# Six blocks of a two-layer trunk take four Strassen pairs in a row instead of one and then two, and one mixer block fetches its decay rows with priority

## The chip, the cores and the metric

The kernel runs on one core of a Trainium2 chip. The metric is the time of one launch in microseconds (us) on the device, the median of three runs. The core has TensorE (PE: matmuls; PEld: its weight loads), VectorE (DVE), ScalarE (ACT), GpSimd (POOL) and SyncE (SP). DMA transfers are issued from queues of SP, POOL and ACT and share 16 DMA engines.

## The reference

256 tokens of width 2048 pass through two layers in fp32. Layer 0 has a combined input projection whose columns feed an mLSTM group (8 heads) and a Mamba-2 group (32 heads), then one output projection. Layer 1 is attention with rotary embedding, 16 heads. Each layer ends in a SwiGLU FFN of width 5632. Cut to the shape of it:

```python
p = rms_norm(x, g1) @ w_in               # q, k, v, o, gates, z, xBC, dt
x = x + concat(mlstm(p), ssd(p)) @ w_out # layer 0
h = rms_norm(x, g2)
x = x + (silu(h @ w_gate) * (h @ w_up)) @ w_down
q, k, v = split(rms_norm(x, g3) @ w_qkv) # layer 1
x = x + attention(rope(q), rope(k), v) @ w_o
h = rms_norm(x, g4)
x = x + (silu(h @ w_gate2) * (h @ w_up2)) @ w_down2
out = rms_norm(x, g5)
```

## The kernel before

All large products have the activations on one side (256 tokens, two tiles of 128) and a weight matrix read from HBM on the other. Both sides are split into a high part (a cast to the matmul's type) and a low part (the number minus its high part), and a product is three matmuls: high by high, high by low, low by high (L311, L312, L313). So each weight tile passes ACT (cast into `wh`, L278) and DVE (low part into `wl`, L283).

The unit of work is `block()`: two strips of 512 columns by 2048 rows, as eight pairs of 256 rows. A pair is done in one of two ways, by its letter in `PLAN`:

- **P**, plain: two raw tiles of 512 KB (`raw`, issued on SP at L270 and L274), two casts, two low parts, 24 matmuls of 128x512.
- **S**, Strassen (Winograd's form): seven products of three matmuls, 21. Besides the first raw tile (L270) and a half-size second one (L272) it needs a tile of weight sums (`sums`): two plain copies on SP (L268), and behind each an accumulating copy on POOL's queue (L269). DVE adds the sums into the second raw (L293), and that into half of the first (L295). Casts and low parts are made of the first raw (a), the sums (s), the second raw (b) and the half (t). The matmuls go in the order of the products 2, 1, 3, 7, 5, 6, 4; the first two use a, the third b.

An S pair also needs sums of its activations: `activation_sums` (four subtractions on DVE, L246 to L249, into `sf`), then a split of `sf` into the tile `sk` (cast on ACT at L145, low part on DVE at L146). They are made when the activations are turned (`transpose_split`), where the list of a tensor names the pair, and else when first asked for (`summed`).

The pools set how far the weights run ahead (`SPACE`): six `raw`, two `sum`, six `wh`, six `wl`. The copies of a sums tile are tied behind the first raw load of five pairs earlier. Weights are emitted at a raised priority of 800. The order of the instructions on each engine is set when the program is built, by a scheduler that goes by priorities and dependences; on the chip each engine and each queue keeps that order.

The blocks follow each other so: bc (two), xz0 to xz3 (Mamba's x and z), qk0, w1 (half of the output projection), v0, o0, qk1, v1, o1, w2, the FFN, av0, aq0, aq1, av1, aq2, aq3 (values, and queries with keys, of layer 1), wo, the FFN. `o` is the plan of both o0 and o1; `aq` that of aq0 to aq3. From here on S4 is pair 4 of a block done as S, P7 pair 7 done as P.

While one block's matmuls run, small tasks of the stage before (`later`, run by `tick`) are put between the pairs: the mLSTM's chunks, the scan, attention's heads. From a block's first S to its last no such task is started. Among them `fetched_rows` (L657) reads decay rows back from a scratch tensor in HBM: two copies into a tile `rows`, on POOL's queue, or on ACT's (`nc.scalar`) where a caller says so. DVE adds masks to them (L671), ACT takes their exponents (L676, L677). Matmuls p_xs (L716) and p_y (L746) belong to that scan.

Of the kernel before, what the change touches and what calls it, by code (L numbers as in the profile page):

```python
# [17 lines left out]
P = 128  # L18
T = 256
# [16 lines left out]
SPACE = {"raw": 6, "sum": 2, "wh": 6, "wl": 6, "xa": 8, "sk": 3, "s": 10, "vh": 2, "ph": 1}  # L36
PLAN = {
    "bc": "PPPPPPPP", "xz": "PPPPPPPP", "qk0": "PPPPPPPP", "w1": ("PSPSPSPP", "PSPSPSSP"),
    "v0": "PPPSPSSP", "o": "PPPSPSSP", "qk1": "PPPSPSSP", "v1": "PPPSPSSP", "w2": ("PPPSPSPP", "PPPSPSSP"),
    "x": "PSPSPSSP", "x0": "PPPSPSSP", "down4": ("PSPSPSSP", "PSPSPSSP"), "down3": ("PSPSPP", "PSPSPP"),  # L40
    "av0": "PPPSPSSP", "aq": "PPPSPSSP", "av1": "PPPSPSSP", "wo": ("PPPPPPPP", "PPPSPSSP"),
}


# [17 lines left out]
def hybrid_trunk(ctx: ExitStack, tc: tile.TileContext, a: dict, out: bass.AP):  # L62
    nc = tc.nc
# [16 lines left out]
    def home(tag):  # L80
        return lambda shape, name, dt=F32: big.tile(shape, dt, tag=tag, name=name, bufs=SPACE[tag])

    xa_home, sk_home, s_home, vh_home = home("xa"), home("sk"), home("s"), home("vh")
    ph_home = home("ph")

    def t2(shape, name, dt=F32):
        return tmp.tile(shape, dt, tag="tmp", name=name, bufs=9)
# [42 lines left out]
    G_MIX0, G_FFN0, G_MIX1, G_FFN1, G_ML, G_SS, G_CB = 0, 16, 32, 48, 64, 80, 96  # L130
# [32 lines left out]
    def later(wait, name, fn, *args):  # L163
        pending.append((clock[0] + wait, len(pending), name, fn, args))
# [21 lines left out]
    def need(name):  # L186
        if any(q[2] == name for q in pending):
            assert not held[0], name
            run_until(lambda p: not any(q[2] == name for q in pending))
# [198 lines left out]
    def gathered(F, pre):  # L388
        for i in (0, 2, 1, 3):
            if pre is None:  # L390
                yield i // 2, i % 2, F[i]
            else:
                with tc.high_priority(offset=1600):
                    added[0] = (nc.vector.tensor_sub if i == 2 else nc.vector.tensor_add)(pre[i], F[i], pre[i]).ins
                yield i // 2, i % 2, pre[i]

    def sumsq(acc, src):
        j = t2([P, src.shape[-1]], "sq")
        nc.scalar.activation(j, src, AF.Square, accum_out=acc)
# [30 lines left out]
    def first_pair(src, turns_after, warm):  # L430
        raw = []
        for w, col in src:
            raw.append(home("raw")([P, 2, STRIP], "raw"))
            for k in range(2):
                nc.sync.dma_start(raw[-1][:, k, :], w[k * P:(k + 1) * P, col:col + STRIP])
        b = xt0.pair(0)
        pt = aux_bank("p_tr")
        with tc.issue_after(turns_after):
            for i in range(2):
                for t in range(NT):  # L440
                    turned = nc.tensor.transpose(pt[:, i * T + t * P:i * T + (t + 1) * P],
                                                 xin[t][:, i * P:(i + 1) * P], ident).ins
        with tc.issue_after(turned):
            warm_up(warm)
        pair = pt.rearrange("p (a b) -> p a b", a=2)
        high = [home("wh")([P, 2, STRIP], "wh", F32R) for _ in raw]
        low = [home("wl")([P, 2, STRIP], "wl", F32R) for _ in raw]

        def staged(s, k):
            with tied(last[0], cast[0]):  # L450
                split(high[s][:, k, :], low[s][:, k, :], raw[s][:, k, :])
            cast[0], last[0] = fresh

        for k in range(2):
            g = pv[:, G_MIX0 + k:G_MIX0 + k + 1]
            with tied(last[0], cast[0]) if k else ExitStack():
                split(b[:, k, 0, :], b[:, k, 1, :], pair[:, k, :], g)
            cast[0], last[0] = fresh
            staged(0, k)
        for k in range(2):  # L460
            staged(1, k)
        return [[(h[:, k, :], l[:, k, :]) for k in range(2)] for h, l in zip(high, low)]
# [57 lines left out]
    with tc.high_priority(offset=2000):  # L520
        first = first_pair(((w_in, C_B), (w_in, C_C)), rows_turned, WARM[1])
# [72 lines left out]
    scr = drp.tile([SH + MH, T], F32, name="scr")  # L594
# [65 lines left out]
    def fetched_rows(first, home, queue=nc.gpsimd):  # L660
        need("gates")
        rb = home([P, 2, W3], "rows2")
        for lo, l0, n in ((0, 0, T), (T, P, P)):
            queue.dma_start(rb[:, :, lo:lo + n],
                            bass.AP(tensor=scr.tensor, offset=scr.offset + first * T + l0,
                                    ap=[[0, P], [T, 2], [1, n]]))
        return rb

    def masked(rb):
# [49 lines left out]
    def ssd_rows(s, j, y, zg, wait=1):  # L719
        rows = fetched_rows(MH + 8 * s + 2 * j, s_home if j % 2 else sk_home, nc.scalar if s == 3 else nc.gpsimd)  # L720
        later(wait, ("y", s), ssd_decay, s, j, rows, y, zg)
# [188 lines left out]
    def next_x(name, gcol, sums, waits=(1, 2, 1, 2)):  # L910
        nx = KT("x" + name, KD, xa_home, sums)
        nx.sums = {j: None for j in sums}
        ss = cst.tile([P, NT, 4], F32, name="ss" + name)

        def done(s):
            cs = slice(s * STRIP, (s + 1) * STRIP)
            turn_strip(nx, s, [xr_[t][:, cs] for t in range(NT)], gcol, waits[s])
            for t in range(NT):
                sumsq(ss[:, t, s:s + 1], xr_[t][:, cs])

        return nx, ss, done
# [58 lines left out]
            down(hT, first, n, first + n == DFF // STRIP)  # L980
            first += n

    xt2, ss2, finish_ffn0 = next_x("2", G_MIX1, {3: sk_home, 5: sk_home, 6: sk_home})
    ffn(xt1, r1, a["l0_ffn_gate"], a["l0_ffn_up"], a["l0_ffn_down"], "a", finish_ffn0)


# [13 lines left out]
    aq, av, prob = {}, {}, {}  # L1000

    def rope_block(g, plan):
        F, pre = block(((w_qkv, g * STRIP), (w_qkv, D + g * STRIP)), xt2, 0, plan)
        tok = {}
        for t, i, src in gathered(F, pre):
            rot = t2([P, STRIP], "rot")
            both = src.rearrange("p (h f) -> p h f", f=HALF)
            nc.vector.tensor_mul(rot.rearrange("p (h f) -> p h f", f=HALF), both,
                                 rope[:, t, 0:1, :].to_broadcast([P, 8, HALF]))
            swp = t2([P, STRIP], "swp")  # L1010
            s4 = src.rearrange("p (h e f) -> p h e f", e=2, f=HALF)
            nc.vector.tensor_mul(swp.rearrange("p (h e f) -> p h e f", e=2, f=HALF), s4[:, :, ::-1, :],
                                 rope[:, t, None, 1:3, :].to_broadcast([P, 4, 2, HALF]))
            nc.vector.tensor_add(rot, rot, swp)
            tok[i, t] = rot
        for i in range(2):
            aq[g, i] = (vh_home if i == 0 else s_home)([P, 4, T], f"aq{i}")
        for i in (1, 0):
            for j in range(2):
                later(2, ("aq", g), qk_pair, aq[g, i][:, 2 * j:2 * j + 2, :],  # L1020
                      [tok[i, t][:, j * T:(j + 1) * T] for t in range(NT)])
        for hh in range(4):
            later(3 + hh // 2, ("oh", g, hh // 2), attend, g, hh)

    def values(g, plan):
        F, pre = block(((w_qkv, 2 * D + 2 * g * STRIP), (w_qkv, 2 * D + (2 * g + 1) * STRIP)), xt2, 0, plan)
        for i in range(2):
            av[2 * g + i] = s_home([P, NT, STRIP], f"av{i}")
        for t, i, src in gathered(F, pre):
            with tc.high_priority(offset=1600 if pre is None else 400):  # L1030
                nc.scalar.activation(av[2 * g + i][:, t, :], src, AF.Copy, scale=r2[:, t:t + 1])
# [42 lines left out]
            split(ob[:, hh % 2, 0, :], ob[:, hh % 2, 1, :], po[:, :T])  # L1074

    values(0, PLAN["av0"])
    rope_block(0, PLAN["aq"])
    rope_block(1, PLAN["aq"])
    values(1, PLAN["av1"])
    rope_block(2, PLAN["aq"])  # L1080
    rope_block(3, PLAN["aq"])
    xt3, ss3, done3 = next_x("3", G_FFN1, {1: vh_home, 3: vh_home, 5: sk_home, 6: ph_home})

    project(a["l1_w_o"], 0, oT, PLAN["wo"], done3)
# [110 lines left out]
```

## Time and profile before

| | us |
|---|---|
| median of 3 runs | 2530.19 (2529.63 to 2530.41) |
| profiled execution | 2527.28 |
| its span | 2525.3 |
| TensorE busy | 2514.8 (100%) |
| its weight loads busy | 2088.2 (83%) |
| DVE busy | 2237.2 (89%) |
| ACT busy | 1593.5 (63%) |
| POOL busy | 360.7 (14%) |
| mean granted clock | 0.999 |

The span runs from the first to the last instruction that the profiler saw; the profiled execution's time has 2.0 us around it and lies 2.9 us under the median of the runs. Busy times of engines overlap. A matmul's busy time counts from its start to its modelled end, and the next one starts before that, so TensorE's rate is read from starts.

### The profile page before, as it was taken

How to read it: one execution, taken by the hardware profiler on the slowest of the kernel's cores; microseconds unless marked ns; L12 is line 12 of the kernel's file. 1: busy time of each engine (PE TensorE's matmuls, PEld its weight loads, DVE VectorE, ACT ScalarE, POOL GpSimd, SP SyncE). 2: the span in 40 equal slices, each digit the busy share in tenths (PEclk: the TensorE clock that was granted, in tenths of full speed). 3: DMA queues.
4: the chain of work that ended last, by engine and by line, in shares of the span. 5: the costliest groups of instructions: out<-in, count | busy, mean ns of one | idle time of the engine just before them, and what ended most of it. 6: DMA issues, size and time to landing. Idle time of an engine off the chain costs nothing.

```text
span 2525.3 us, 34564 instructions
## 1 busy us (share of the span) xinstructions
PE 2514.8 (100%) x11553; PEld 2088.2 (83%) x11553; DVE 2237.2 (89%) x2984; ACT 1593.5 (63%) x2161; POOL 360.7 (14%) x444
## 2 busy tenths in 40 slices
PE   9999999999999999999999999999999999999998
PEld 8888888888888888888888888888888888888887
DVE  6877788978789999999999989988899999999998
ACT  6566666576767666566566666657666656665665
POOL 2101101121111111111111111110011111111110
PEclk9999999999999999999999999999999999999999
DMA  8656669878788999999999878776689999999995
GB/s 283 186 168 185 198 198 263 269 226 263 216 233 249 287 266 282 281 289 263 287 282 283 263 235 243 239 225 208 194 249 279 266 285 282 273 277 290 296 265 180
DMA packets 335362, 631.52 MB, mean 250 GB/s; under 512 B 27288, under 2 KB 31904, under 8 KB 335184
## 3 DMA queue, kind: packets, MB, share of 16 engines
q1 hardware_dynamic: 278960, 527.71, 61.8%
q0 software_dynamic: 52864, 98.18, 22.0%
q10 hardware_dynamic: 3360, 3.42, 0.5%
q8 instruction: 91, 1.49, 0.2%
q14 instruction: 87, 0.71, 0.1%
HBM read 627.07 MB, written 2.14 MB: 249 GB/s over the span
## 4 chain that ended last, share of the span: by engine, by line
PE 97%; DVE 1%; DMA 1%; ACT 0%; issue 0%; SPq 0%; POOL 0%; POOLq 0%; DVEq 0%; ACTq 0%
PE acc_f L311 24%; PE acc_f L313 24%; PE acc_f L312 24%; PE acc_e L311 6%; PE acc_e L313 6%; PE acc_e L312 6%; PE p_tr L178 1%; PE p_y L746 1%; PE p_qt L178 0%; PE p_o L178 0%; PE p_num L836 0%; DVE wl L283 0%; ACT wh L278 0%; PE p_qk L1038 0%; DMA raw<-in_l_w_in 0%
## 5 line engine op out<-in xcount | busy, mean ns | idle before, releaser
L278 ACT CAST wh<-raw 128x1024 fp32r<-128x1024 f32 (+1 forms) x1084 | 1047.2, 982 | 646.4 <-PE acc_f L313 278.4
L283 DVE TENSOR_TENSOR wl<-raw,wh 128x1024 fp32r<-128x1024 f32 (+1 forms) x1084 | 1208.8, 1135 | 161.3 <-ACT wh L278 151.1
L311 PE MATMUL acc_f<-wh,x 128*128 128x512 f32 x1168 | 457.5, 392 | 0.0
L313 PE MATMUL acc_f<-wh,x 128*128 128x512 f32 x1168 | 455.1, 390 | 0.0
L312 PE MATMUL acc_f<-wl,x 128*128 128x512 f32 x1168 | 454.8, 389 | 0.0
L278 ACT CAST wh<-sums 128x1024 fp32r<-128x1024 f32 x174 | 182.9, 1051 | 148.5 <-PE acc_f L313 72.5
L311 PE MATMUL acc_f<-wh,xa 128*128 128x512 f32 x678 | 269.6, 398 | 0.1
L313 PE MATMUL acc_f<-wh,xa 128*128 128x512 f32 x678 | 264.9, 391 | 0.0
L312 PE MATMUL acc_f<-wl,xa 128*128 128x512 f32 x678 | 264.6, 390 | 0.1
L313 PEld LDWEIGHTS acc_f<-wh,x 128*128 128x128 f32 x1168 | 219.2, 188 | 46.2
L312 PEld LDWEIGHTS acc_f<-wl,x 128*128 128x128 f32 x1168 | 219.4, 188 | 45.0
L311 PEld LDWEIGHTS acc_f<-wh,x 128*128 128x128 f32 x1168 | 219.3, 188 | 44.7
L283 DVE TENSOR_TENSOR wl<-sums,wh 128x1024 fp32r<-128x1024 f32 x174 | 212.3, 1220 | 31.8 <-ACT wh L278 30.9
L311 PE MATMUL acc_e<-wh,sk 128*128 128x512 f32 x522 | 203.6, 390 | 0.1
L312 PE MATMUL acc_e<-wl,sk 128*128 128x512 f32 x522 | 203.6, 390 | 0.0
L313 PE MATMUL acc_e<-wh,sk 128*128 128x512 f32 x522 | 203.4, 390 | 0.0
L269 POOL DMA_DIRECT2D sums<-in_l_ffn_gate x86 | 74.3, 864 | 773.1 <-DMA sums<-in_l_ffn_up 363.1
L313 PEld LDWEIGHTS acc_f<-wh,xa 128*128 128x128 f32 x678 | 127.3, 188 | 27.2
L312 PEld LDWEIGHTS acc_f<-wl,xa 128*128 128x128 f32 x678 | 127.5, 188 | 25.9 <-DVE wl L283 0.5
L311 PEld LDWEIGHTS acc_f<-wh,xa 128*128 128x128 f32 x678 | 127.3, 188 | 25.0 <-ACT wh L145 0.3
L293 DVE TENSOR_TENSOR raw<-raw,sums 128x512 f32<-128x512 f32 x174 | 119.3, 685 | 13.6 <-DMA sums<-in_l_ffn_down 7.5
L295 DVE TENSOR_TENSOR raw<-raw 128x512 f32<-128x512 f32 x174 | 119.5, 687 | 2.0
(334 smaller groups left out, 4034.4 us busy)
## 6 DMA issues: line engine op xcount, KB each, us to landing
raw<-in_l_ffn_gate SPq DMA_DIRECT2D x176, 512.0 KB, 6.2
raw<-in_l_w_in SPq DMA_DIRECT2D x175, 512.0 KB, 4.7
raw<-in_l_ffn_down SPq DMA_DIRECT2D x136, 512.0 KB, 6.8
raw<-in_l_ffn_up SPq DMA_DIRECT2D x90, 512.0 KB, 5.8
sums<-in_l_ffn_up SPq DMA_DIRECT2D x172, 256.0 KB, 5.0
raw<-in_l_w_qkv SPq DMA_DIRECT2D x78, 512.0 KB, 6.0
raw<-in_l_w_out SPq DMA_DIRECT2D x52, 512.0 KB, 6.0
sums<-in_l_ffn_gate POOLq DMA_DIRECT2D x86, 256.0 KB, 6.6
```

What stands on the lines that cost most here:

```text
L178: chain[kind] = put(*args, **kw).ins
L269: nc.gpsimd.dma_start(sums[:, i, :], other, accum_op=OP.add)
L278: cast[0] = nc.scalar.copy(h[:, :n, :], of[:, :n, :]).ins
L283: last[0] = nc.vector.tensor_sub(l[:, :n, :], of[:, :n, :], h[:, :n, :].bitcast(F32)).ins
L293: nc.vector.tensor_add(b[:, 1, :], b[:, 0, :], sums[:, 0, :])
L295: nc.vector.tensor_add(a[:, 0, :], a[:, 0, :], b[:, 1, :])
L311: nc.tensor.matmul(dst, ah, bh, start=start, stop=False, **kw)
L312: nc.tensor.matmul(dst, ah, bl, start=False, stop=False, **kw)
L313: nth[0] = nc.tensor.matmul(dst, al, bh, start=False, stop=stop, **kw).ins
L746: nc.tensor.matmul(py[:, o0:o0 + SHD], e[:, lo:lo + P], y[:, st, hs], start=st == 0, stop=st == t, skip_group_check=True)
```

## The change

It has three edits. The plans of o (two blocks), v1, av0, aq0 and aq2 get an S in the place of the P of pair 4, so that pairs 3, 4, 5 and 6 are S in a row. Since the blocks of layer 1 now differ, `aq` is written out as aq0 to aq3. The activations of layer 1's attention get a home for the sums of pair 4, so that these are made when the activations are turned. And `fetched_rows` gives its copies a priority of 1200 where they go on ACT's queue, which the last of the x and z blocks (xz3) does.

```diff
@@ PLAN
-    "v0": "PPPSPSSP", "o": "PPPSPSSP", "qk1": "PPPSPSSP", "v1": "PPPSPSSP", "w2": (...),
+    "v0": "PPPSPSSP", "o": "PPPSSSSP", "qk1": "PPPSPSSP", "v1": "PPPSSSSP", "w2": (...),
-    "av0": "PPPSPSSP", "aq": "PPPSPSSP", "av1": "PPPSPSSP", ...
+    "av0": "PPPSSSSP", "aq0": "PPPSSSSP", "aq1": "PPPSPSSP", "av1": "PPPSPSSP",
+    "aq2": "PPPSSSSP", "aq3": "PPPSPSSP", ...
@@ fetched_rows
         for lo, l0, n in ((0, 0, T), (T, P, P)):
-            queue.dma_start(rb[:, :, lo:lo + n], ...)
+            with tc.high_priority(offset=1200 if queue is nc.scalar else 0):
+                queue.dma_start(rb[:, :, lo:lo + n], ...)
@@
-    xt2, ss2, finish_ffn0 = next_x("2", G_MIX1, {3: sk_home, 5: sk_home, 6: sk_home})
+    xt2, ss2, finish_ffn0 = next_x("2", G_MIX1, {3: sk_home, 4: vh_home, 5: sk_home, 6: sk_home})
```

At the end `rope_block(0, PLAN["aq"])` and its three sisters become `rope_block(0, PLAN["aq0"])` and so on.

What this moves on the engines is shown at three places. First SP's queue in o0, before, from P4's two raws on: P4, S5's raws, S6's sums, S6's raws, P7 (L268 x2 are the two plain copies of one tile of sums).

```order
L270 DMA raw<-in_l_w_in 128x2x512
L274 DMA raw<-in_l_w_in 128x2x512
L270 DMA raw<-in_l_w_in 128x2x512
L272 DMA raw<-in_l_w_in 128x512
L268 DMA sums<-in_l_w_in 128x512 x2
L270 DMA raw<-in_l_w_in 128x2x512
L272 DMA raw<-in_l_w_in 128x512
L270 DMA raw<-in_l_w_in 128x2x512
L274 DMA raw<-in_l_w_in 128x2x512
```

The same queue at that place now: S4's raws, S5's raws, S5's sums, S6's raws, S6's sums, P7.

```order
L270 DMA raw<-in_l_w_in 128x2x512
L272 DMA raw<-in_l_w_in 128x512
L270 DMA raw<-in_l_w_in 128x2x512
L272 DMA raw<-in_l_w_in 128x512
L268 DMA sums<-in_l_w_in 128x512 x2
L270 DMA raw<-in_l_w_in 128x2x512
L272 DMA raw<-in_l_w_in 128x512
L268 DMA sums<-in_l_w_in 128x512 x2
L270 DMA raw<-in_l_w_in 128x2x512
L274 DMA raw<-in_l_w_in 128x2x512
```

S5's sums stood further up before, and S6's stood ahead of S6's raws; now S5's stand there, and S6's behind S6's raws.

Second DVE in av0, before: the first row ends the sums of pair 6's activations (`sk`). Behind it stand the rest of S5 and all of S6, with the split of pair 7's activations (`x_13601`) in between; P7 is next.

```order
L146 TENSOR_TENSOR sk<-sf,sk 128x4x128
L295 TENSOR_TENSOR raw<-raw 128x512
L283 TENSOR_TENSOR wl<-sums,wh 128x1024
L283 TENSOR_TENSOR wl<-raw,wh 128x1024
L283 TENSOR_TENSOR wl<-raw,wh 128x512
L293 TENSOR_TENSOR raw<-raw,sums 128x512
L283 TENSOR_TENSOR wl<-raw,wh 128x1024
L146 TENSOR_TENSOR x_13601<-xg,x_13601 128x2x256
L295 TENSOR_TENSOR raw<-raw 128x512
L283 TENSOR_TENSOR wl<-sums,wh 128x1024
L283 TENSOR_TENSOR wl<-raw,wh 128x1024
L283 TENSOR_TENSOR wl<-raw,wh 128x512
```

DVE in av0 now, from S6's first addition on:

```order
L293 TENSOR_TENSOR raw<-raw,sums 128x512
L283 TENSOR_TENSOR wl<-sums,wh 128x1024
L295 TENSOR_TENSOR raw<-raw 128x512
L283 TENSOR_TENSOR wl<-raw,wh 128x1024
L283 TENSOR_TENSOR wl<-raw,wh 128x512
L283 TENSOR_TENSOR wl<-raw,wh 128x1024 x2
L247 TENSOR_TENSOR sf<-xg 128x128
L283 TENSOR_TENSOR wl<-raw,wh 128x1024 x2
L248 TENSOR_TENSOR sf<-xg,sf 128x128
L146 TENSOR_TENSOR x_13655<-xg,x_13655 128x2x256
L249 TENSOR_TENSOR sf<-xg,sf 128x128
L146 TENSOR_TENSOR sk<-sf,sk 128x4x128
```

Three of the four subtractions of pair 6's activation sums and their split (`sk`, last row), and the split of pair 7's activations (`x_13655`), stand behind S6, P7 (the first x2) and aq0's first pair (the second x2). Before they stood ahead of S5's rest and within S6. On TensorE 12 matmuls of S6 and 14 of P7 follow that last split.

Third ACT's queue at the end of xz3, where the row fetches are issued (L664 before, L665 now; L696 and L697 of before are L697 and L698 now). Before:

```order
L664 DMA rows_2937<-scr 128x2x256
L696 ACTIVATE thz<-acc_f,rh_553 128x512
L697 ACTIVATE zg<-acc_f,rh_553 128x512
L278 CAST wh<-raw 128x1024
L148 ACTIVATE sx_2913<-p_tr,pv 128x256
L278 CAST wh<-raw 128x1024
L664 DMA rows_2937<-scr 128x2x128
L148 ACTIVATE sx_2913<-p_tr,pv 128x256
L664 DMA rows_3004<-scr 128x2x256
L664 DMA rows_3004<-scr 128x2x128
L278 CAST wh<-raw 128x1024
L479 ACTIVATE cv<-p_cv,convb,phase 128x256 x2
```

And now:

```order
L665 DMA rows_2937<-scr 128x2x256
L697 ACTIVATE thz<-acc_f,rh_553 128x512
L698 ACTIVATE zg<-acc_f,rh_553 128x512
L665 DMA rows_2937<-scr 128x2x128
L665 DMA rows_3077<-scr 128x2x256
L665 DMA rows_3077<-scr 128x2x128
L278 CAST wh<-raw 128x1024 x2
L148 ACTIVATE sx_2913<-p_tr,pv 128x256
L665 DMA rows_3004<-scr 128x2x256
L665 DMA rows_3004<-scr 128x2x128
L665 DMA rows_3135<-scr 128x2x256
L665 DMA rows_3135<-scr 128x2x128
```

The fetches of the first two tiles stand together ahead of two casts of weights, and those of the other two follow a few rows on; before, a cast, a split (L148) and another cast stood between the two copies of the first tile.

More of the change, by code (lines that the diff above doesn't have):

```diff
@@ L38 @@
     "bc": "PPPPPPPP", "xz": "PPPPPPPP", "qk0": "PPPPPPPP", "w1": ("PSPSPSPP", "PSPSPSSP"),
-    "v0": "PPPSPSSP", "o": "PPPSPSSP", "qk1": "PPPSPSSP", "v1": "PPPSPSSP", "w2": ("PPPSPSPP", "PPPSPSSP"),
+    "v0": "PPPSPSSP", "o": "PPPSSSSP", "qk1": "PPPSPSSP", "v1": "PPPSSSSP", "w2": ("PPPSPSPP", "PPPSPSSP"),
     "x": "PSPSPSSP", "x0": "PPPSPSSP", "down4": ("PSPSPSSP", "PSPSPSSP"), "down3": ("PSPSPP", "PSPSPP"),
-    "av0": "PPPSPSSP", "aq": "PPPSPSSP", "av1": "PPPSPSSP", "wo": ("PPPPPPPP", "PPPSPSSP"),
+    "av0": "PPPSSSSP", "aq0": "PPPSSSSP", "aq1": "PPPSPSSP", "av1": "PPPSPSSP", "aq2": "PPPSSSSP", "aq3": "PPPSPSSP", "wo": ("PPPPPPPP", "PPPSPSSP"),
 }
@@ L663, in fetched_rows @@
         for lo, l0, n in ((0, 0, T), (T, P, P)):
-            queue.dma_start(rb[:, :, lo:lo + n],
-                            bass.AP(tensor=scr.tensor, offset=scr.offset + first * T + l0,
-                                    ap=[[0, P], [T, 2], [1, n]]))
+            with tc.high_priority(offset=1200 if queue is nc.scalar else 0):
+                queue.dma_start(rb[:, :, lo:lo + n],
+                                bass.AP(tensor=scr.tensor, offset=scr.offset + first * T + l0,
+                                        ap=[[0, P], [T, 2], [1, n]]))
         return rb
@@ L1076, in hybrid_trunk @@
     values(0, PLAN["av0"])
-    rope_block(0, PLAN["aq"])
-    rope_block(1, PLAN["aq"])
+    rope_block(0, PLAN["aq0"])
+    rope_block(1, PLAN["aq1"])
     values(1, PLAN["av1"])
-    rope_block(2, PLAN["aq"])
-    rope_block(3, PLAN["aq"])
+    rope_block(2, PLAN["aq2"])
+    rope_block(3, PLAN["aq3"])
     xt3, ss3, done3 = next_x("3", G_FFN1, {1: vh_home, 3: vh_home, 5: sk_home, 6: ph_home})
```

## The prediction

> **What bounds the kernel now.** I read the page's busy lines and its chain first, then the waits of TensorE, then the chain of one attention block, then the groups and the copies of one block.
>
> ```profile
> span 2525.3 us, 34564 instructions
> PE 2514.8 (100%) x11553; PEld 2088.2 (83%) x11553; DVE 2237.2 (89%) x2984; ACT 1593.5 (63%) x2161; POOL 360.7 (14%) x444
> q1 hardware_dynamic: 278960, 527.71, 61.8%
> q0 software_dynamic: 52864, 98.18, 22.0%
> PE 97%; DVE 1%; DMA 1%; ACT 0%; issue 0%; SPq 0%; POOL 0%; POOLq 0%; DVEq 0%; ACTq 0%
> ```
>
> TensorE is the bound from end to end, VectorE (DVE) is next with 89%, and the DMA engines are busy for 84% of their time. So every matmul taken out pays its full price, as long as nothing makes TensorE wait. Today it hardly waits at all:
>
> ```profile
> PE p_xs L716 <- DVE xs L490: 1.0, 1, 1.0
> PE warm L122 <- POOL phase L105: 1.0, 1, 1.0
> ```
>
> A matmul's own 390 ns overlaps its neighbours, so its price is read from the chain, which counts from start to start. These are the first and the last of 45 matmuls in a row in pair 1 and pair 2 of the second attention block (aq0):
>
> ```profile
> 1504.78 0.23 PE acc_f L311
> ...
> 1514.76 0.23 PE acc_f L313
> ```
>
> They lie 44 steps apart, (1514.76 − 1504.78)/44 = 0.2268 us. A P pair (24 matmuls) is 5.44 us of TensorE, an S pair (21) 4.76.
>
> What an S pair asks of the other engines is in the groups (mean ns is the last number before the second bar):
>
> ```profile
> L283 DVE TENSOR_TENSOR wl<-raw,wh 128x1024 fp32r<-128x1024 f32 (+1 forms) x1084 | 1208.8, 1135 | 161.3 <-ACT wh L278 151.1
> L278 ACT CAST wh<-sums 128x1024 fp32r<-128x1024 f32 x174 | 182.9, 1051 | 148.5 <-PE acc_f L313 72.5
> L283 DVE TENSOR_TENSOR wl<-sums,wh 128x1024 fp32r<-128x1024 f32 x174 | 212.3, 1220 | 31.8 <-ACT wh L278 30.9
> L293 DVE TENSOR_TENSOR raw<-raw,sums 128x512 f32<-128x512 f32 x174 | 119.3, 685 | 13.6 <-DMA sums<-in_l_ffn_down 7.5
> L295 DVE TENSOR_TENSOR raw<-raw 128x512 f32<-128x512 f32 x174 | 119.5, 687 | 2.0
> ```
>
> A P pair has two low parts of 1.22 us on DVE (the 1135 mixes in half-size ones), 2.44. An S pair has three of 1.22, a half-size one of 0.69 and two additions of 0.69: 5.72. So an S pair takes DVE 0.96 us longer than TensorE, and four in a row plus P7 need 4 × 5.72 + 2.44 = 25.3 us of DVE beside 4 × 4.76 + 5.44 = 24.5 of TensorE.
>
> **Part 1, matmuls removed.** Six pairs P→S, three matmuls each: 18 × 0.2268 = −4.08 us, all on the bound.
>
> **Part 2, the third S in a row and its copies.** Each new S adds two plain copies and two accumulating ones. There are two sum buffers, so pair 6's copies start when DVE has made the low part of pair 4's sums. Before, they started after pair 3's. Here is the buffer's cycle for pair 6 of aq0: issue and landing, then cast and low part, then the pair's first matmul (first start is the first time in each row):
>
> ```profile
> L268 SPq DMA_DIRECT2D sums<-in_l_w_qkv x2: 341/384/426, 1507.2 to 1507.6; - x2
> L269 POOL DMA_DIRECT2D sums<-in_l_w_qkv x2: 862/1040/1217, 1510.6 to 1511.1; - x2
> DMA to landing us min/median/max: 2.8/5.3/8.1
> ...
> L278 ACT CAST wh<-sums x1: 1053/1053/1053, 1525.3 to 1525.3; 128x1024 fp32r<-128x1024 f32 x1
> L283 DVE TENSOR_TENSOR wl<-sums,wh x1: 1224/1224/1224, 1526.3 to 1526.3; 128x1024 fp32r<-128x1024 f32 x1
> ...
> L311 PE MATMUL acc_f<-wh,x x2: 389/389/389, 1529.8 to 1533.9; 128*128 128x512 f32 x2
> ```
>
> The last accumulate is issued at 1511.1 and lands 8.1 later, at 1519.2: 12.0 us after the first issue. Today that is harmless, since the cast comes only at 1525.3. The shortest such cycle that I found in these blocks is pair 6 of qk1:
>
> ```profile
> L268 SPq DMA_DIRECT2D sums<-in_l_w_in x2: 340/382/425, 551.0 to 551.4; - x2
> L269 POOL DMA_DIRECT2D sums<-in_l_w_in x2: 862/1039/1216, 554.2 to 554.7; - x2
> DMA to landing us min/median/max: 2.6/4.0/5.9
> ```
>
> That is 554.7 + 5.9 − 551.0 = 9.6 us. I take 10.9, between the two, where most of the others also lie. Now the new cycle, with T3 for pair 3's first matmul. The sums' low part ends 1526.3 + 1.2 = 1527.6, 2.2 before its pair. The cast before it waits for a wh buffer, of which six exist, so pair 4's cannot come much earlier. It ends at T3 + 4.76 − 2.2 = T3 + 2.5. Pair 6's copies then land at T3 + 2.5 + 10.9 = T3 + 13.4. Behind that stand cast 1.05, low part 1.22 of the sums, addition 0.69, low part 1.22 of the second raw: T3 + 17.6. Pair 6 would start at T3 + 14.3 and has six matmuls (1.36) that do without: T3 + 15.7. **TensorE waits 1.9 us** in a block where nothing else is late (0.6 by 9.6, 3.0 by 12.0).
>
> DVE's load tells the blocks apart. These are the five last pairs of o0, v1, o1, av0, aq0 and aq2 (each row: stretch, its length, then busy time of TensorE, its loads and DVE):
>
> ```profile
> 515.90:540.80 24.90, 24.90 (x111) 20.64 (x110) 22.32 (x26) 17.42 (x22) 4.27 (x5) 1.00 0.77 233
> 603.90:629.00 25.10, 25.10 (x114) 20.76 (x113) 22.17 (x26) 15.80 (x18) 3.46 (x4) 1.00 0.85 252
> 651.90:677.00 25.10, 25.10 (x112) 20.77 (x111) 21.57 (x29) 18.43 (x32) 4.54 (x5) 1.00 0.73 226
> 1473.30:1498.30 25.00, 25.00 (x112) 20.67 (x112) 24.47 (x30) 18.09 (x24) 3.56 (x4) 1.00 0.82 249
> 1514.80:1539.80 25.00, 25.00 (x112) 20.69 (x111) 21.44 (x24) 16.17 (x17) 3.48 (x4) 1.00 0.92 271
> 1657.20:1682.20 25.00, 25.00 (x112) 20.71 (x111) 21.47 (x24) 16.17 (x17) 3.54 (x4) 1.00 0.85 252
> ```
>
> Each gains 5.72 − 2.44 = 3.28 us of DVE and loses 0.68 of TensorE. In aq0 and aq2 that makes 24.7 beside 24.3, which a lead of a few us covers: only the copies count, 2.2 in aq0 (its DMA share is 0.92 already) and 1.6 in aq2; bounds 0.4 and 3. In v1 and o1 DVE was idle for 2.9 and 3.5 us. v1 enters pair 3 with much of its weights made, so I take 0.5 (0 to 1.7). o1 has other DVE work in the way: 1.4 (0.7 to 2.2). In o0 the sums of pair 4's activations, four subtractions and two splits that the change puts ahead of S4's first low part, move pair 4's sums to about T3 + 4.9: 2.4 later than in the clean case, so 1.9 + 2.4 = 4.3 less a little that the late TensorE gives back, 4.1 (3.0 to 5.5).
>
> **Part 3, av0.** This block is the dear one. DVE is busy for 24.47 of 25.0 us there, and the order puts the rest of pair 6's activation sums, and the split of the activations of pair 7, behind all weights of av0 and of aq0's first pair. Durations of that chain:
>
> ```profile
> L146 DVE TENSOR_TENSOR sk<-sf,sk x2: 685/685/685, 1474.2 to 1478.5; 128x512 fp32r<-128x512 f32 x2
> L249 DVE TENSOR_TENSOR sf<-xg,sf x1: 284/284/284, 1475.4 to 1475.4; 128x128 f32<-128x128 f32 x1
> L145 ACT CAST sk<-sf x3: 617/621/623, 1465.4 to 1476.9; 128x512 fp32r<-128x512 f32 x3
> ```
>
> Say pair 4's sums are done at 1477.3 (T3 + 4.0; clean it would be 1475.8). Then DVE has S4's rest with the split of pair 6's activations and one subtraction (2.9), S5 (5.7), S6 (5.7), P7 (2.4), a subtraction (0.3), aq0's first pair (2.4), two subtractions and pair 7's split (1.3): 20.7 in all, 1498.0. Pair 6's copies land at 1477.3 + 10.9 = 1488.2, when DVE stands at S6's first addition at about 1487: another 1 us. Then ScalarE casts sk (0.6): sk is there at about 1499.2. TensorE has run all that it can ahead of it and still has 26 matmuls (12 of pair 6, 14 of pair 7), 5.9 us: aq0 starts at 1505.1 where it started at 1498.5. With Part 1's 0.7 that is a wait of 7.3 us. Lower bound: with pair 4 clean and copies in time the same chain ends about 3 earlier, 4.3. Upper bound, by 12.0 us of copies and aq0's banks freed later, 10.
>
> **Part 4, the row fetches.** They move up on ScalarE's queue, past casts. The wait they could touch:
>
> ```profile
> 311.12 4.50 DMA rows<-scr
> ...
> 329.05 0.70 DVE xs L490
> 329.88 0.63 PE p_xs L716 x4
> ```
>
> The 4.50 us of this transfer is in the chain of that one wait, but ahead of 329.05 lie a sums copy, a cast and a low part too. A fetch started earlier also puts its masks (L671) earlier on DVE, ahead of low parts that TensorE needs, and the p_xs matmuls now stand after pair 3's first ones, 3 to 4 us later. I take 0: −1.2 if the wait goes, +1 if DVE is delayed by as much.
>
> **Sum.** −4.1 + o0 4.1 + v1 0.5 + o1 1.4 + av0 7.3 + aq0 2.2 + aq2 1.6 + rows 0 = +13.0. The profiled execution took 2527.28 (span 2525.3 and 2.0 around it); it becomes 2540.3. The median of the runs lies 2.9 above it, so 2543.2 in the metric. All lower ends together, −4.1 + 3.0 + 0 + 0.7 + 4.3 + 0.4 + 0.4 − 1.2 = +3.5, give 2533.7. All upper ends, −4.1 + 5.5 + 1.7 + 2.2 + 10 + 3 + 3 + 1 = +22.3, give 2552.5.
>
> **A rule against the row.** The page lists how long the copies take from issue to landing (the last number is the median):
>
> ```profile
> sums<-in_l_ffn_up SPq DMA_DIRECT2D x172, 256.0 KB, 5.0
> sums<-in_l_ffn_gate POOLq DMA_DIRECT2D x86, 256.0 KB, 6.6
> ```
>
> Together that is 11.6 us. The Trainium skill, "DMA: Bandwidth & Descriptors", section "Anatomy of one DMA — SWDGE (gpsimd) path", fits a GpSimd copy as about 2.0 us plus its bytes over 436 GB/s, which for 256 KB is an estimate of 2.6 us, and 5.2 for a plain one and an accumulating one behind it. By that rule no copy would be late in any block. The trace disagrees, with 6.6 for the accumulate alone in a loaded queue, and the sum above goes by the rows.
>
> **Rivals.**
> *Copies in time* (it decides where the cycle stays below 10.9 − 1.9 = 9.0 us). For it: a starved TensorE asks for fewer bytes, and the DMA share is 0.73 to 0.85 in five of the six blocks. Against it: no cycle that I followed was under 9.6. Then only DVE's load costs: o0 1.0, o1 0.6, av0 4.3, so −4.1 + 5.9 = +1.8: 2532.0, not told from no change. The formula of the Trainium skill's page cited above leads here.
> *All covered* (not slower): pair 6's sk chain is overtaken by nothing that matters, because TensorE's lead in weights lets DVE reach it before its pair; this decides if av0's DVE has 5 us of lead at pair 3. The four S pairs then cost what the matmuls cost, −4.1, and with the p_xs wait gone −5.2: 2525.0 to 2526.1. Against it: 24.47 of 25.0 us.
> *Copies under load*: an extra S pair moves more bytes on the slower queue (22.0% of the DMA time for 98.18 MB, where q1 has 61.8% for 527.71). If the cycle becomes 14 us, each of the six blocks waits 3.1 more than at 10.9, +18: 2561.
> *The change does nothing*: excluded for Part 1, since the matmuls are gone from TensorE's order; possible for Part 4, which is in the sum as 0.
>
> **How the numbers follow.** Chances: the forecast's case 0.62 (own range 2533.7 to 2552.5), copies in time 0.18, all covered 0.09, copies under load 0.11. 0.2% is 5.1 us, about what a measurement of this kernel tells from no change: under 2525.1 is faster, over 2535.3 slower. All covered straddles the lower limit, so faster gets 0.05 of it and the rest, 0.04, is no change. To that come 0.16 of copies in time and 0.07 of the forecast's case, its lower end: 0.27. What is left, 0.68, is slower. The range leaves out the lower part of all covered and most of copies under load: 2528 to 2554.
>
> **What would show it.** In the changed profile: TensorE's waits list the low part L283 or its additions in o0, o1, aq0 and aq2, once per block near pair 6, some 2 us each, and pair 6's cast follows its landing at once. In av0 one wait of 4 us or more on the activation split L145 or L146, and aq0 starts about 6.6 us later against av0's pair 3 than now. TensorE shows 18 matmuls fewer. I am wrong if the waits of av0 are under 3 us (then DVE had a lead that I did not see), or if the clean blocks wait nothing (then the copies were short, or the sums of pair 4 came earlier than T3 + 2.5).

## The result: 2559.99 us against 2530.30, slower by 1.2%, and the profile after

The changed kernel takes 2559.99 us (median of 4 runs, 2555.96 to 2562.55) where the kernel before took 2530.30 beside it (2529.63 to 2530.61). The ratio is 1.0116, with an interval of 1.0099 to 1.0134. The prediction said slower, 2543.2, within 2528 to 2554: the direction was right, the size is more than twice what was forecast, outside the range. The four runs spread over 6.6 us and the four of the kernel before over 1.0; since a later set of 21 runs of the kernel before spread over 6.7, nothing is read from that.

The profiled execution took 2555.96 us, 28.7 more than that of before. Its page, and TensorE's waits in it (total, times, longest):

```profile
span 2554.2 us, 34644 instructions
PE 2522.9 (99%) x11535; PEld 2087.1 (82%) x11535; DVE 2257.6 (88%) x3019; ACT 1602.3 (63%) x2175; POOL 371.4 (15%) x456
PE 86%; DVE 5%; DMA 4%; issue 2%; ACT 1%; POOL 1%; POOLq 0%; DVEq 0%; SPq 0%; ACTq 0%
```

```profile
PE acc_f L312 <- DVE wl L283: 8.4, 9, 1.6
PE acc_f L311 <- ACT wh L278: 5.5, 5, 3.5
PE acc_e L311 <- ACT xg L237: 2.4, 1, 2.4
PE acc_f L313 <- DVE x L146: 2.2, 1, 2.2
PE p_xs L717 <- DVE xs L490: 1.9, 1, 1.9
PE warm L122 <- POOL phase L105: 1.0, 1, 1.0
PE p_qt L178 <- DVE rot L1015: 0.8, 2, 0.5
PE acc_f L311 <- DVE xin L887: 0.2, 1, 0.2
```

18 matmuls are gone (11553 to 11535), 4.1 us of work, and yet TensorE is busy for 8 us more. That is no wait: some 5 us of it are slow matmuls, shown below, and the rest was not taken apart. Where two rows stood before there are now eight, and TensorE's share of the chain fell from 97% to 86%.

Comparing the start of each block in both traces tells where the 28.7 us went. Each number is how much later the next block starts, net of the 0.68 that three fewer matmuls save:

| stretch | forecast, net | measured |
|---|---|---|
| row fetches (xz3, qk0) | 0 | 0.84 |
| o0 | 3.4 | 3.89 |
| v1 | −0.2 | 0.83 |
| o1 | 0.7 | 1.19 |
| av0 to the start of aq0 | 6.6 | 12.10 |
| aq0 | 1.5 | 3.79 |
| aq2 | 0.9 | 3.84 |
| blocks behind these (0.85 in aq1, 0.55 in aq3, 0.6 in the last FFN) | 0 | about 2 |

Pair 6 of aq0, after: the sums copies, then their cast and low part (first start is the first time in a row).

```profile
L268 SPq DMA_DIRECT2D sums<-in_l_w_qkv x2: 328/396/463, 1536.9 to 1537.3; - x2
L269 POOL DMA_DIRECT2D sums<-in_l_w_qkv x2: 862/1038/1214, 1540.5 to 1541.1; - x2
DMA to landing us min/median/max: 2.7/4.5/7.5
...
L278 ACT CAST wh<-sums x1: 1049/1049/1049, 1548.7 to 1548.7; 128x1024 fp32r<-128x1024 f32 x1
L283 DVE TENSOR_TENSOR wl<-sums,wh x1: 1225/1225/1225, 1549.8 to 1549.8; 128x1024 fp32r<-128x1024 f32 x1
```

Pair 3 started at 1534.36, so the copies were issued at T3 + 2.5, as forecast. They landed at 1541.1 + 7.5 = 1548.6, 11.7 us later, and the cast began 0.1 after that; before, the cast came 6 us after the landing. The chain of that window shows what stood behind it:

```profile
1541.07 7.53 DMA sums<-in_l_w_qkv
...
1548.70 1.06 ACT wh L278
...
1549.79 1.23 DVE wl L283
1551.01 0.60 DVE raw L295
1551.61 0.80 DVE wl L283
```

TensorE, which began pair 6 at 1548.64, did its six matmuls and waited till 1550.75 and again till 1552.80, 2.57 us in all. Then something came that the forecast did not have. Pair 6 in the two traces, stretch by stretch, before and after (behind the length: busy time of TensorE, its loads, DVE, ACT, POOL; then the granted clock):

```profile
1529.78:1534.54 4.76, 4.76 (x22) 3.94 (x21) 4.22 (x5) 4.15 (x5) 0.86 (x1) 1.00 1.04 337
```

```profile
1548.64:1557.71 9.07, 6.93 (x22) 5.03 (x21) 7.62 (x8) 6.98 (x8) 1.75 (x2) 0.81 0.90 243
```

The pair took 9.07 us instead of 4.76, and TensorE was busy for 6.93 of them with the same matmuls: the clock granted there was 0.81. Single matmuls tell it too, those behind the wait against those of the next product and pair:

```profile
L311 PE MATMUL acc_e<-wh,sk x3: 632/632/632, 1553.4 to 1556.0; 128*128 128x512 f32 x3
L311 PE MATMUL acc_f<-wh,x x2: 393/395/397, 1557.0 to 1557.7; 128*128 128x512 f32 x2
```

632 ns instead of 390, and 0.427 us from start to start instead of 0.227, for about 3 us. That is 1.7 us more in aq0, as much in aq2, and 1.4 at the end of av0.

### The profile page after: what moved, and what is told of

It reads as the page before. It is cut to its first block, busy times and chain, and to the rows that moved or that the text cites. A ratio compares the mean times of both kernels' runs of the same rounds, so it can differ in the third digit from the quotient of the medians.

```text
span 2554.2 us, 34644 instructions
## 1 busy us (share of the span) xinstructions
PE 2522.9 (99%) x11535; PEld 2087.1 (82%) x11535; DVE 2257.6 (88%) x3019; ACT 1602.3 (63%) x2175; POOL 371.4 (15%) x456
## 4 chain that ended last, share of the span: by engine, by line
PE 86%; DVE 5%; DMA 4%; issue 2%; ACT 1%; POOL 1%; POOLq 0%; DVEq 0%; SPq 0%; ACTq 0%
PE acc_f L313 22%; PE acc_f L312 22%; PE acc_f L311 21%; PE acc_e L311 6%; PE acc_e L313 6%; PE acc_e L312 6%; DVE wl L283 3%; PE p_tr L178 1%; DMA raw<-in_l_w_qkv 1%; ACT wh L278 1%; PE p_y L747 1%; DMA raw<-in_l_w_in 1%; DMA sums<-in_l_w_qkv 1%; DMA sums<-in_l_ffn_down 1%; DMA sums<-in_l_w_in 0%
## 5 line engine op out<-in xcount | busy, mean ns | idle before, releaser
L278 ACT CAST wh<-raw 128x1024 fp32r<-128x1024 f32 (+1 forms) x1090 | 1049.1, 980 | 651.9 <-PE acc_f L313 274.7
L283 DVE TENSOR_TENSOR wl<-raw,wh 128x1024 fp32r<-128x1024 f32 (+1 forms) x1090 | 1212.1, 1133 | 151.9 <-ACT wh L278 142.1
L311 PE MATMUL acc_f<-wh,x 128*128 128x512 f32 x1150 | 451.4, 393 | 4.3 <-ACT wh L278 3.9
L313 PE MATMUL acc_f<-wh,x 128*128 128x512 f32 x1150 | 448.2, 390 | 2.2 <-DVE x L146 2.2
L312 PE MATMUL acc_f<-wl,x 128*128 128x512 f32 x1150 | 448.5, 390 | 0.0
L278 ACT CAST wh<-sums 128x1024 fp32r<-128x1024 f32 x180 | 189.1, 1050 | 156.0 <-PE acc_f L313 62.1
L311 PE MATMUL acc_f<-wh,xa 128*128 128x512 f32 x660 | 262.7, 398 | 0.0
L312 PE MATMUL acc_f<-wl,xa 128*128 128x512 f32 x660 | 257.6, 390 | 1.0 <-DVE wl L283 1.0
L313 PE MATMUL acc_f<-wh,xa 128*128 128x512 f32 x660 | 258.0, 391 | 0.0
L311 PEld LDWEIGHTS acc_f<-wh,x 128*128 128x128 f32 x1150 | 216.2, 188 | 50.9 <-ACT wh L278 4.7
L313 PEld LDWEIGHTS acc_f<-wh,x 128*128 128x128 f32 x1150 | 215.9, 188 | 48.2 <-DVE x L146 2.9
L283 DVE TENSOR_TENSOR wl<-sums,wh 128x1024 fp32r<-128x1024 f32 x180 | 219.6, 1220 | 39.2 <-ACT wh L278 38.9
L311 PE MATMUL acc_e<-wh,sk 128*128 128x512 f32 x540 | 212.3, 393 | 0.1
L312 PE MATMUL acc_e<-wl,sk 128*128 128x512 f32 x540 | 211.8, 392 | 0.0
L313 PE MATMUL acc_e<-wh,sk 128*128 128x512 f32 x540 | 211.6, 392 | 0.0
L313 PEld LDWEIGHTS acc_f<-wh,xa 128*128 128x128 f32 x660 | 123.9, 188 | 26.4
L311 PEld LDWEIGHTS acc_f<-wh,xa 128*128 128x128 f32 x660 | 124.1, 188 | 24.3 <-DVE pre L394 0.3
```

The costliest lines, as they stand in the source:

```text
L278: cast[0] = nc.scalar.copy(h[:, :n, :], of[:, :n, :]).ins
L283: last[0] = nc.vector.tensor_sub(l[:, :n, :], of[:, :n, :], h[:, :n, :].bitcast(F32)).ins
L311: nc.tensor.matmul(dst, ah, bh, start=start, stop=False, **kw)
L312: nc.tensor.matmul(dst, ah, bl, start=False, stop=False, **kw)
L313: nth[0] = nc.tensor.matmul(dst, al, bh, start=False, stop=stop, **kw).ins
```

## The experiments

Theory 1 is the forecast's: the third S in a row makes pair 6's copies late. Its rival, theory 2, is DVE's load: an S pair costs DVE 5.72 us beside TensorE's 4.76, wherever it stands. Then there were three questions of size: the half pace, the row fetches, and av0. All medians below stand beside runs of the kernel before on the same chip, 2529.5 to 2530.3.

**The row fetches.** First the plans alone, without the priority:

```diff
-            with tc.high_priority(offset=1200 if queue is nc.scalar else 0):
+            with ExitStack():
```

> The changed plans without the row fetches' priority. In the changed kernel's trace TensorE waits 2.25 us (start to start) for the scan's p_xs where it was 1.40 before, and qk0 to w1 lost 0.84 us. If the fetches are the cause, this kernel is 0.8 us faster than the changed one (about 2559) and the wait is back at 1.40. Rival: the fetches do nothing and the loss is a chance of that execution, then it equals the changed kernel, 2560.

2563.0 us (2558.0 to 2567.0). The total does not resolve 0.8 us. In its trace the stretch from qk0 to w1 lost 0.13 us instead of 0.84.

The priority alone, on the kernel before (the same line the other way round):

> The kernel before with the row fetches' priority alone. By the trace of the changed kernel: +0.8 us, 2531.1. By the forecast's middle: 0, 2530.3. If an earlier fetch takes the p_xs wait away: -1.2, 2529.1.

2530.56 us, ratio 1.0000 with 0.9992 to 1.0009: not told from no change. In its trace the stretch lost 0.70. Of the ten traces with the priority eight show 0.7 to 2.9 there and two 0.3; of the three without it two show about 0.1 and one (the combined kernel below) 0.8. The two pairs of traces that differ by the priority alone both differ by 0.7, so it most likely costs that much; since as much was also lost once without it, this is not shown. It gains nothing in any record.

**The half pace.** The changed kernel with matmuls of zeros in the wait:

```diff
+                    if p == 3 and j == last_s:
+                        for _ in range(fill):   # 11 in aq0 and aq2
+                            with tied(nth[0]):
+                                nth[0] = nc.tensor.matmul(F[0], zero, b11[0], start=False, stop=False).ins
```

> The changed kernel, and in aq0 and aq2, between product 1 and product 3 of pair 6, 11 matmuls each with a tile of zeros, which add nothing to the result and need nothing that is late. They cost 11 x 0.227 = 2.5 us of TensorE and lie in a wait that was 2.57 and 2.49 us there. Theory A, a wait is followed by matmuls at half pace (0.427 us from start to start instead of 0.227; 1.7 us more in each of the two blocks): with TensorE kept busy the pace stays 0.227 and the kernel gets 3 to 3.5 us faster, 2556.5 to 2557. Theory B, the slow matmuls behind the wait have another cause (weights that come in one by one): nothing gained, 2560, or slower by what sticks out of the wait.

2561.53 us: the total shows no gain. In the trace no matmul of aq0 or aq2 ran at half pace, and these blocks lost 2.93 and 2.71 us instead of 3.79 and 3.84; but aq1 behind aq0 lost 4.96 instead of 0.85. It also shows nothing certain about the blocks, since in the run of the plans alone aq0 and aq2 ran at full pace too, with waits of 3.28 and 2.55 us and nothing in them (aq0's is shown, from its pair's sixth matmul on; the granted clock is 1.00):

```profile
1553.00:1560.50 7.50, 4.65 (x19) 3.28 (x18) 6.72 (x7) 6.47 (x8) 1.75 (x2) 1.00 0.79 183
```

The weights came in late there just as in the changed kernel, so their lateness alone does not make the slow pace. Eight traces have pair 6 of v1, aq0 and aq2 in the order of the changed kernel. 16 of these pairs waited 2.2 us or more, and 13 of them went on at half pace; of the 8 that waited less (two of them with the zeros in the wait), none did. That holds for these three blocks only. In the same eight traces pair 6 of o0 waited 2.7 to 3.4 us, in three parts, and only one went on at half pace. In the changed kernel it did not, with 3.4 us of wait:

```profile
532.28:540.70 8.42, 5.62 (x22) 3.79 (x21) 7.36 (x8) 6.38 (x8) 1.75 (x2) 1.00 0.97 249
```

So the length of the wait alone does not decide, and what else does was not found.

**Where the fourth S stands.** The changed kernel with pair 2 in the place of pair 4:

```diff
-PPPSSSSP   next_x("2", ..., {3: sk_home, 4: vh_home, 5: sk_home, 6: sk_home})
+PPSSPSSP   next_x("2", ..., {2: vh_home, 3: sk_home, 5: sk_home, 6: sk_home})
```

> The changed kernel with the fourth S at pair 2 instead of pair 4 in all six blocks (PPSSPSSP, the activations' sums of pair 2 in place of those of pair 4): the same matmuls, copies and DVE work, but pair 6's sums buffer is again freed by pair 3, three pairs earlier. Theory 1, the copies of the third S in a row are late: pair 6 waits for nothing in o0, v1, o1, aq0, aq2, each block is 0.7 shorter than before; with av0 still a few us late the time is 2527 to 2534. Theory 2, DVE's load of four S pairs is the cause wherever they stand: still 2550 or more.

2533.71 us, ratio 1.0018 (1.0009 to 1.0027). The same matmuls, copies and DVE work cost 26 us less in another order. Its waits:

```profile
PE p_xs L717 <- DVE xs L490: 2.4, 1, 2.4
PE p_qt L178 <- DVE rot L1015: 2.2, 2, 1.8
PE p_tr L178 <- DVE pre L879: 2.1, 2, 1.4
PE warm L122 <- POOL phase L105: 1.0, 1, 1.0
PE acc_e L311 <- ACT xg L237: 0.6, 1, 0.6
PE acc_f L312 <- DVE wl L283: 0.4, 2, 0.2
```

The waits for weights are gone but for 0.4 us. o0, v1, o1, aq0 and aq2 are shorter than before by 0.21, 0.42, 0.97, 0.68 and 0.58 us, and av0 loses 1.05. What is left of the loss lies in tasks behind them: 2.76 in w2a behind o1, 2.61 in aq1 behind aq0, 1.35 at the fetches.

**A third sums buffer.**

```diff
-SPACE = {"raw": 6, "sum": 2, ...}   tmp bufs=9
+SPACE = {"raw": 6, "sum": 3, ...}   tmp bufs=7
```

> The changed kernel with three sums buffers instead of two; the room comes from the pool of temporaries (7 instead of 9). Pair 6's copies then wait for pair 3's low part again, as before the change. Theory 1 (late copies): the waits at pair 6 of v1, aq0, aq2 go (1.4, 2.6, 2.5 us and the half pace behind them), those of o0 and av0 shrink to what DVE's load leaves; about 2543 to 2548 if seven temporaries cost nothing. Theory 2 (DVE's load of an S pair, 5.72 us beside 4.76 of TensorE): the waits stay within 0.5 us of what they were, 2558 or more.

2543.2 us, ratio 1.0052 (1.0036 to 1.0069), as theory 1 had it. v1 and aq0 are now shorter than before, by 0.68 and 0.51 us; aq2 loses 0.84 and o0 0.71. o1 loses 1.86, more than before the third buffer. av0 hardly moved, it lost 10.85:

```profile
PE acc_f L313 <- DVE x L146: 2.8, 1, 2.8
PE acc_e L311 <- ACT xg L237: 2.8, 1, 2.8
PE acc_f L312 <- DVE wl L283: 2.5, 5, 1.2
```

The first two rows are av0's. Of the third, 1.5 us lie at S5 of o1, 0.4 in av0, 0.2 in o0 and 0.4 in the kernel's first block. From S3 to P7 nothing waits any more in v1, aq0 and aq2; what aq2 loses lies in its first pairs. So late copies make the waits of v1, aq0 and aq2 and most of o0's, and DVE's load of four S pairs does not. o1 is different already in the changed kernel: its main wait (1.1 us) is at S5, and pair 6's sums were cast 1.4 us after they had landed, where the other five blocks cast them after 0.1. What remains in o0 and o1 is laid to DVE's load, which no run shows apart. The seven temporaries may have a part in it: in the combined kernel below, o1 with its plan as before lost 0.67. av0 is another matter.

**av0.** First its plan as before, the rest as changed:

```diff
-    "av0": "PPPSSSSP"
+    "av0": "PPPSPSSP"
```

> The changed kernel with av0's plan as before (the sums of pair 4's activations are still made there, for aq0 and aq2). By the trace av0 and the start of aq0 lost 12.1 us: about 2548. If it is the making of pair 4's activation sums that costs, and not av0's own fourth S, most of the loss stays: 2556 or more.

2547.89 us, and av0 lost 1.66: its own fourth S costs the rest of the 12.1, some 10 us. The changed trace shows an idle stretch of DVE in it, and what ended it. Here is the idle stretch before and after, and the chain after:

```profile
DVE phase L995 <- POOL r L141: 1.7, 1, 1.7
...
DVE phase L996 <- POOL r L141: 2.5, 1, 2.5
...
1476.55 0.18 DVE rs L140
1476.73 0.49 POOL sums L269
1477.27 1.22 POOL sums L269
1478.48 0.75 POOL r L141
1479.26 0.04 DVE phase L996
```

DVE stands at the scaling of the rotary table, which needs a small power on GpSimd. That stands on POOL's queue behind S5's two accumulating copies, whose plain ones had to wait for a sums buffer. The stand is not new: before, it was 1.7 us, and no S pair of av0 waited. The power itself takes 1.4 of it; what has grown is its wait in the queue, from 0.2 us to 1.1. Writing the scaling behind the block was to take DVE out of it:

```diff
-    for t in range(NT): nc.vector.tensor_scalar(rope[:, t], ...)   # behind r2 = norm_of("2", ss2)
+    for t in range(NT): nc.vector.tensor_scalar(rope[:, t], ...)   # behind values(0, PLAN["av0"])
```

> The changed kernel with the two scalings of the rotary table (L996 on DVE, which need the norm that GpSimd's L141 makes) put behind the block av0. In the changed kernel DVE stood 2.5 us at the first of them, since L141 stood on POOL's queue behind the accumulating copies of S5, which wait for their plain copies; TensorE then waited 2.83 us (start to start) at S3 of av0. If that is the cause: this wait goes, av0 is 2.5 us shorter and the kernel about 2557.5. If av0's late weights decide anyway, the wait only moves to S6: no change, 2560. Read from the trace of av0, since the total varies by more.

2559.29 us, and av0 lost 11.17. This run tells nothing: the scheduler put the first scaling where it had been, and DVE stood at it for 3.0 us. So it was tied:

```diff
+    with tied(last[0]):
         for t in range(NT): nc.vector.tensor_scalar(rope[:, t], ...)
```

> The changed kernel with the two scalings of the rotary table tied behind the last weights of av0 on DVE, so that DVE cannot stand there for GpSimd's L141 (the run that only wrote them later left them where they stood). If that stand started av0's loss: the wait of 2.83 us (start to start) at S3 of av0 goes, and av0 with the start of aq0 loses 9 to 10 us instead of 12.1. If the split of pair 7 and pair 6's sums behind all weights decide alone: the loss stays at 11 to 12, with a later, longer wait at S6 and P7.

2555.62 us; av0 lost 7.01 instead of 12.10. S3's wait is gone (2.73 us of it), and pair 6 lost 6.11 instead of 8.36. The tie moved three of pair 6's four subtractions forward as well. But the split of its sums and that of pair 7's activations stand behind all weights of av0 and of aq0's first pair still, as in the changed kernel (where they started at 1511.6 and 1510.1):

```profile
L146 DVE TENSOR_TENSOR sk<-sf,sk x1: 685/685/685, 1510.6 to 1510.6; 128x512 fp32r<-128x512 f32 x1
L146 DVE TENSOR_TENSOR x<-xg,x x1: 683/683/683, 1511.2 to 1511.2; 128x512 fp32r<-128x512 f32 x1
```

So these 5 us came without the splits' place. Next the splits and sums were put forward by priority:

```diff
+                with tc.high_priority(offset=1600 if kt.name == "x2" else 0):
                     split(...); kt.sums[j] = activation_sums(xg, kt.sum_home[j])
```

> The changed kernel with a priority of 1600 on the splits and activation sums of layer 1's attention input, so that on DVE pair 6's sums and pair 7's split stand ahead of S5's weights again, as before the change. If their place made av0's loss, as the forecast has it: the waits on L146 and L237 go, and av0 with the start of aq0 loses 2 to 4 us (pair 6's late copies with what follows them), the kernel takes about 2551. If DVE's load in av0 (24.47 us busy of 25 before) makes it, whatever the order: 9 us or more are still lost, 2557.

2556.29 us; av0 lost 6.43, between the two expectations, with no wait at S3. Here the norm and the scaling had moved backward as well, behind the block, so DVE did not stand either. So a last one with the norm and the scaling ahead of them (priority 1700):

> The two last runs each moved two things in av0 on DVE: the scaling of the rotary table (which stands for GpSimd's L141) went behind the block, and pair 6's sums with pair 7's split went ahead of S5. Here the splits and sums keep their priority of 1600 and the norm and its scaling get 1700, so the scaling stands ahead of S4's weights again and only the splits are early. If DVE's stand at the scaling makes the 5 us by which both runs were better in av0: TensorE waits 2 us or more at S3 of av0 again and av0 with the start of aq0 loses 10 us or more (7.0 and 6.4 without the stand). If the place of the splits and sums makes them: it loses 6 to 8.

2558.0 us; av0 lost 8.97, but not where either expectation looked. The norm now came early enough for the POOL queue to be free, DVE stood for 0.6 us, S3 waited for nothing and pair 6 lost 5.42. Instead the block's first pair waited (2.6 us from start to start) for residual sums on DVE (L888), with half pace behind it: 4.2 lost there. The expectation had a premise wrong: in the run with the tie the two splits had not moved ahead of S5. What the runs show together is this. Over the traces with av0's fourth S at pair 4, S3 lost 2.7 to 4.0 us where DVE stood 2.5 to 3.0, and nothing where it stood 0.6 or less. Without the stand pair 6 loses 5.4 to 6.1 us instead of 8.4, whether the splits are late (6.1) or early (5.8 and 5.4). So the stand goes with some 5 us of av0's loss, and the splits' place alone with less than 1. It is one trace for each, and why 1.7 us of stand did no harm before is not shown; the sums of pair 4's activations, which now stand on DVE there, are the likeliest reason, since the kernel with av0's plan undone still has them and lost 1.6 at S3. What stays in pair 6 is its late copies: in all three runs their cast came 0.1 us after the landing.

**All together**, without o and the fetches (12 matmuls fewer):

```diff
 four S in a row in v1, av0, aq0, aq2; sum 3, tmp 7; splits of "x2" at 1600; scaling tied behind av0; no row priority
```

> A candidate: four S in a row in v1, av0, aq0 and aq2 alone (o as before, 12 matmuls less), no row priority, three sums buffers, seven temporaries, the activation splits of layer 1 first, the rotary scaling behind av0. By theory 1 nothing waits in v1, aq0 and aq2 and av0 loses at most 3 us: 2528 to 2532, not told from the kernel before. If av0's load decides whatever the order: 2536 or more.

2533.95 us, ratio 1.0014 (1.0005 to 1.0023): slower than expected by 2, and not faster than before. But the four S in a row of av0 now run without any wait from S3 to P7, which are 0.68 us shorter than before, and so do v1, aq0 and aq2:

```profile
PE acc_f L312 <- DVE xin L888: 1.9, 1, 1.9
PE p_xs L718 <- DVE xs L491: 1.8, 1, 1.8
PE p_o L178 <- DVE prob L1040: 1.3, 1, 1.3
PE acc_f L312 <- DVE pre L395: 1.0, 1, 1.0
```

No row of weights (L283's or L278's kind) is left. What is lost is at the blocks' starts: 3.8 us at av0's first pair, again the residual sums with half pace behind them, 1.3 in aq0 (pre), 1.5 in aq2's first pairs. Three things were changed for av0 at once here (the third buffer, the early splits, the tie), so which of them it needs was not tried.

**More of it.** Nine blocks as PPSSPSSP, on the kernel before:

```diff
 "v0", "o0", "qk1", "v1", "aq0", "aq1", "av1", "aq2", "aq3": "PPPSPSSP" -> "PPSSPSSP"; xt2.sum_home[2] = vh_home
```

> The kernel before, no row priority, with PPSSPSSP in nine blocks (v0, o0, qk1, v1, aq0, aq1, av1, aq2, aq3); o1 and av0 as before, and layer 1's sums of pair 2 made when first asked for, in aq0, and not in av0. 27 matmuls less. Theory 1: -6.1 if nothing waits, 2524; in the run with six such blocks each was 0.2 to 0.7 us shorter but two tasks behind them were 2 to 3 us late, so 2524 to 2529. Theory 2: slower than 2530.

2574.94 us, ratio 1.0182 (1.0167 to 1.0197): theory 1's expectation, 2524 to 2529, failed by 46 us or more. The first S of aq1 took 16.6 us, that of av1 22.8.

```profile
PE p_qt L178 <- DVE rot L1015: 15.6, 4, 5.4
PE acc_f L312 <- DVE wl L283: 5.2, 4, 2.9
PE acc_f L311 <- ACT wh L278: 3.8, 6, 1.0
PE p_pt L178 <- ACT prob L1052: 3.0, 2, 2.1
```

The rotation and the softmax of the block before must pass DVE and ACT within the pairs ahead of the first S, since no task is started from there on. With two P pairs instead of three, in block after block, they do not. v0, with no attention ahead of it, lost 9.1. Theory 2 had expected a slower kernel here; whether DVE's load alone would make it was not tried apart.

No kernel that ran was faster than the one before.

## Why the prediction was wrong

Two steps failed: av0's sum left out S3 and what holds DVE ahead of it (5.5 us), and a wait of TensorE was priced at its length, with nothing for the slow matmuls behind it (3.5 us in aq0 and aq2). The smaller misses are the cycle of the copies, the row fetches and the blocks behind.

- **The removed matmuls** are right: where nothing waits, a changed block is 0.68 us shorter (v1 with the third buffer, aq0 with PPSSPSSP).
- **The late copies** are right as a mechanism, nearly to the formula: copies issued at T3 + 2.5, wait = cycle − 9.0. aq0's cycle of 11.7 us gives 2.7, and 2.57 was measured. The cycle of 10.9 was too short: 11.2, 11.8, 10.5, 12.3, 11.7 and 11.6 us in the six blocks. The trace of before had it already: pair 6's cycle was 10.9, 11.7, 11.5, 10.2, 12.1 and 11.0 there, so most lay above the 10.9 that was taken. The upper end, 12.0, held five of the six. The Trainium skill's formula ("DMA: Bandwidth & Descriptors", section "Anatomy of one DMA — SWDGE (gpsimd) path") with its estimate of 5.2 us for the two copies would have had no wait. In aq0 the two plain copies took 2.7 and 3.0 us to land, near its 2.6, but the accumulating ones 6.0 and 7.5, and the traces decide against it here.
- **The missing term** is the half pace. I priced a wait at its length. In v1, aq0 and aq2 TensorE then went on at half pace for about 3 us in 13 cases of 16, 1.7 us each: that makes aq0 and aq2 4.5 us gross where 2.2 and 1.6 were forecast. It differs from trace to trace of the same plans (v1 lost 0.83 in the changed kernel, and 3.6 without the priority, where it had the half pace), so v1's small loss is luck in part. The Trainium skill, "TensorE: Matmul & The Clock Gate", Part 1, states this: a matmul of 512 columns starts every 426.7 ns while the clock is gated, a window of about 3.4 us decides on the gate, and that window runs freely, so that the same kernel is hit differently from run to run at its start. The trace agrees with 0.427 us, and with a difference from run to run in the middle of a kernel too. The Trainium skill, on the same page, section "Why this matters for your kernels", advises to leave no idle gaps over about 3 us; here 2.2 us in two parts were enough in one case, and the measurement decides.
- **av0** was sized at 7.3 gross and lost 12.8. The split of pair 7 on DVE (L146) was there as forecast, but with a wait of 2.2 us and not 4 or more; the longest wait (3.5) was for weights that stood on ACT behind pair 6's casts and so behind its late copies, which I had as "another 1 us" on DVE. I took pair 4's sums at T3 + 4.0, they were done at T3 + 6.1, and S3 itself waited first. I named no wait on POOL's queue, though S5's accumulates and the norm's power both stand on it. S3's loss (2.7), half pace at its end (1.4) and 1.3 lost in its first pair make 5.4 of the 5.5 us missing.
- **o0, o1** came within 0.5 us. In o0 the mechanism held (pair 4's sums at T3 + 4.9, as forecast); o1's number is luck in part, since its main wait was at S5 and not at pair 6's copies. **v1** came within 1.0: 1.5 gross where 0.5 was taken, since the lead that I counted let its copies start only 1.2 us earlier, at T3 + 1.3, and their cycle took 11.8.
- **The row fetches** were taken as 0, and the stretch lost 0.8 in the trace (0.7 alone). The last of the eight copies landed at 324.7 instead of 339.4, and yet TensorE waited 1.9 us for p_xs instead of 1.0; why stays open. The upper end had it.
- **The blocks behind** (2 us) had no term in the sum, and no run looked for their cause.
- **Rivals**: "copies under load" gave 2561 for the wrong reason, a cycle of 14 us. It was 11.5, so that it came near the measured time is luck.

## What to carry to other kernels

A step that is short of one engine's time may still lose by the depth of one small pool: count which release each transfer waits for, and how many steps ahead that is, before counting work. Reordering the same work (26 us here) was worth more than the work removed (4). A wait of TensorE of 2 us or more may cost nearly 2 us beyond its length; take that for the upper end, since here it came in three blocks mostly and in o0 hardly. And look for every small operation that shares an in-order queue with a transfer that waits.

## What the runs showed of the hardware

After waits of 2.2 to 4.5 us in all at pair 6 of v1, aq0 and aq2, TensorE's matmuls ran at 0.427 us from start to start instead of 0.227 for about 3 us, with a granted clock of 0.81 over aq0's pair, in 13 cases of 16; under 2.2 us there in none of 8. In o0 waits of 2.7 to 3.4 us in three parts did that in one case of 8.

A power of two numbers per partition on GpSimd takes 1.4 us by its row. It stood behind two accumulating copies on the same queue and started 1.1 us after its input was ready, and DVE stood for 2.5 us in all until it had the result.

The accumulating copies of 256 KB at pair 6 of aq0 landed 6.0 and 7.5 us after their issue, the plain ones of the same size 2.7 and 3.0 us after theirs.
